# Single PSUM banks, other places and order of loads, six accumulators, and squares added on VectorE in a decoder layer's projections and gate

## The chip, the cores and the metric

One Trainium2 chip, of which the kernel uses one core. A core has TensorE (PE: matrix products; its weight loads, PEld, overlap them), VectorE (DVE), ScalarE (ACT), GpSimd (POOL) and SyncE (SP). TensorE writes its sums to PSUM, eight banks of 128 x 512 float32; VectorE and ScalarE read them from there. SP, POOL and ACT issue DMAs, each from a queue of its own in fixed order. The metric is the device time in microseconds (us) of one execution; less is better.

## What is computed

One layer over 1024 tokens of width 2048: norm, one projection to the columns of two attention groups, attention, output projection with residual, a gated embedding, a last norm. The change lies outside of attention:

```python
hn = rmsnorm(h, norm_mix_g[i])
proj = hn @ w_in[i]
...
mixed = jnp.concatenate([sb_out * jax.nn.silu(sb_g), df_out * jax.nn.silu(df_g)], axis=-1)
h = h + mixed @ w_out[i]
gate = jax.nn.sigmoid(rmsnorm(h, norm_ple_g[i]) @ w_ple_gate[i])
h = h + gate * (p[i] @ w_ple_proj[i])
return rmsnorm(h, norm_final_g)
```

All is float32. Activations lie transposed, features on partitions and 512 tokens (one half of the sequence) in a row, so a row block of 128 features is a tile of 128 x 512.

## The kernel before

**Products.** TensorE multiplies float32r, so each float32 operand is split into a high part (a cast, on ScalarE) and a low part (a subtraction, on VectorE), and each product is three matmuls: high x high, high x low, low x high. A group of four blocks of 128 is twelve matmuls of 128 x 512.

**Seven products for eight.** Three matrices (the columns for values and gates, the output projection, the gate) are multiplied by Winograd's scheme. The activations are cut by half of the tokens and half of the features into A11, A12, A21, A22, the weights likewise; seven products of sums are formed, named after their activation operand: A11, A12, S1 to S4 and A22. Operands S1 to S4 are formed ahead and kept in DRAM; weight sums (T1 to T4) are formed by VectorE from raw blocks 11, 12, 21, 22. For one output block (a unit `u`), A11 and A12 add up in accumulator `a`; S2, then S3 or A22, in `b`; S1, then S4, in `c`. Between, VectorE reads the partial sums: `u2 = b + s1` after S2 (L1225, L1867), `u3 = b + s1` after S3 (L1245, L1890), `o = c + u3` (L1247, L1897); after A22 into `b` and S4 into `c` come the last reads (L1169, L1791). A reader stands between two groups of matmuls into the same accumulator, so the second group waits for it.

**Stages.** To about 633 us: values and gates, 16 units in two phases (`ph`, halves of the features). To about 1655 us: projection of queries and keys, with attention of the previous head beside it. Then the output projection, 8 units in two phases, to about 1998 us; it stores rows of h (`h_d`) and their squares. Then the gate in three passes, where `gprod` (L1914) multiplies with all features at once (24 matmuls) for a unit:

- first pass: `p1(u)` multiplies A11 into accumulator `pa[u]` and stores the sum, `p2(u)` adds A12, and `gate1(u)` multiplies the embedding (`ple`: 6 matmuls into a tile `z`), scales `pa[u]` by the norm (`o`, L1996) and forms the new row of h. The order is written out: p1 0, 1, 2, p2 0, 1, norm, p1 3, p2 2, gate1 0, p1 4, gate1 1, p2 3, and so on.
- second pass: `p6` (S2), `p5` (S1) and `p3` (S4), in the order p6 0, p5 0, then for each u: p6 u+1, p3 u, p5 u+1.
- last pass: S3 and A22 of each unit for the other half of the tokens, with rows `q` and `h` read back from DRAM, the last norm, and the output rows. The tail after unit 5 works in halves of 256 tokens.

**PSUM.** Pool `pp` has two banks with the tag `acc` and two with `t`; pool `pz` has two tiles of two banks each. Attention takes a score tile `z` from it. In the projections one tile of `pz` is both `b` and `c` (L1221, L1862), except in every third unit of the first phase, where b and c are two `acc` tiles; in the gate, a single accumulator takes half of a tile of `pz` and leaves the other half empty. `pa[u]` lies in `acc` for u = 0, 1, 4, 5 and in `pz` for the others (L1979).

**Order.** The instructions of PE, VectorE and ScalarE stand in the order in which the program writes them. Each product is followed by `step()` (L828): it casts one further weight tile (`whigh` on ScalarE, L794; `wlow` on VectorE, L808 or L806), some five tiles ahead of its use, then runs what is due: operand splits from a list `xq` (two in a step), and functions put off by one to three steps (`soon`). Cast weights lie in a ring of ten tiles. DMAs on SP and POOL are ordered by a planner that simulates the program when it is built; `tc.issue_after(ins)` keeps a DMA behind `ins` on its queue.

**Loads of the gate.** Raw weights of the first pass come line by line into two buffers of two blocks (`first_load`, L1691; a line is A11 or A12 of a unit; the load for the line after next is asked for when a line is cast). For the second pass there are two sets of raw blocks; `second_diffs` (L1718) forms the sums of unit u and asks for the blocks of unit u+1, which take the buffers of unit u-1. Operands (8 rows of 256 KB for each name) are loaded where others have been used up: `GPLACE` (L1342) names the places (XP are pairs of tiles that held rows of x or of the projection's operands; FREE1 and FREE2 are attention's tiles v, pt, pt, q and q, k, k2, v2, which the projection's S3 and S1 used last), `NEXT` and `GNEXT` (L1345) the product after which they are asked for, with first row and count; `gate_loads` (L1368) puts their splits into `xq`. The squares of gate rows go to DRAM by a POOL DMA, two sums that accumulate there (`add_squares`, L1377), and are loaded again for the last norm (L2204).

Of the kernel before, what the change touches and what calls it, by code (L numbers as in the profile page):

```python
# [13 lines left out]
F32 = mybir.dt.float32  # L14
# [6 lines left out]
P = 128  # L21
D = 2048
S = 1024
HALF = 512
# [46 lines left out]
def _body(ctx, nc, tc, ap):  # L71
# [552 lines left out]
    with tc.tile_pool(name="at", bufs=2) as at, tc.tile_pool(name="pz", bufs=2, space=PSUM) as pz:  # L624
# [582 lines left out]
        for ph in range(2):  # L1207
            for u in range(2 * H):
# [117 lines left out]
        sq_d = dram.tile([3, 2, P, HALF], F32, name="sq_d", tag="sq_d")  # L1326
        SUMS = "S1", "S2", "S3", "S4"

        def load_operand(ph, nm, i, eng=nc.sync):
# [4 lines left out]
            if src is None:  # L1334
# [40 lines left out]
        nsq = [0, 0, 0, 0]  # L1375

        def add_squares(k, s):  # L1377


            n = nsq[k]  # L1380
            nsq[k] += 1
            G.dma_start(sq_d[k, n % 2], s, **(dict(accum_op=ALU.add) if n > 1 else {}))

        def row_squares(hf, o):
            n = nsq[3]
            nsq[3] += 1
            t = ev.tile([P, HALF], F32, name="rsq", tag=f"rstd{n % 2}", bufs=1)
            A.activation(t, o, AF.Square)
            add_squares(2 * hf, t)
# [79 lines left out]

        for half in (1, 0):  # L1470
# [200 lines left out]
        op.ticks = True  # L1671
        gneg = ev.tile([P, NK], F32, name="gneg", tag="zm", bufs=1)
# [45 lines left out]
        def second_diffs(u, ks):  # L1718
# [26 lines left out]
        for u in range(8):  # L1745
            for nm in ("S2", "S1", "S4"):
# [93 lines left out]
        for ph in range(2):  # L1840
            for u in range(8):
# [16 lines left out]
                elif ph == 1 and u == 7:  # L1858
                    b = pz.tile([P, 2, HALF], F32, name="pbc", tag="z")[:, 0, :]
                    c = None  # L1860
                else:
                    bc = pz.tile([P, 2, HALF], F32, name="pbc", tag="z")  # L1862
                    b, c = bc[:, 0, :], bc[:, 1, :]
# [27 lines left out]
                if ph:  # L1891
                    V.tensor_tensor(u3, u3, r[0, u + 8], op=ALU.add)
                    if u == 7:
                        c = pz.tile([P, 2, HALF], F32, name="pbc", tag="z")[:, 1, :]
# [14 lines left out]
        gate_loads("A12", 4)  # L1909

# [35 lines left out]
        def load_sums(half, tags):  # L1946
            r = []
            for i, (pool, tag, n) in enumerate(tags):
                r.append(pool.tile([P, HALF], F32, name="sums", tag=tag, bufs=n))
# [11 lines left out]
        def gating1(u, c, o, z):  # L1961
# [39 lines left out]
        p1(0)  # L2001
        p1(1)
        p1(2)
        op.calm = False
        embedding_load(1, "f")
        sums2 = load_sums(2, ((ev, "rstd1", 1), (ev, "ssq", 1)))
# [5 lines left out]
        plew_load(0, 0)  # L2012
        plew_load(1, 0)
# [3 lines left out]
        plew(0, 0)  # L2017
# [28 lines left out]
        def p6(u):  # L2046
# [8 lines left out]
            parts2[u] = pz.tile([P, 2, HALF], F32, name="pc", tag="z")[:, 0, :], w  # L2055
# [344 lines left out]
```

## Time and profile before

| | |
|---|---|
| median of 3 runs | 2388.85 us (2388.27 to 2389.63) |
| the profiled execution | 2393.9 us, span 2392.1 us |
| granted TensorE clock, mean | 0.992 |
| DMA | 590.46 MB, 247 GB/s |

By stage (busy us of each engine, and the mean share of the 16 DMA engines):

| stage, us | PE | DVE | ACT | DMA share |
|---|---|---|---|---|
| 53 to 633, values and gates | 574.5 of 580 | 404.1 | 218.8 | 0.88 |
| 633 to 1655, queries, keys, attention | 1007.2 of 1022 | 777.1 | 613.8 | 0.71 |
| 1655 to 1998, output projection | 334.7 of 343 | 273.0 | 149.7 | 0.89 |
| 1998 to 2104, gate, first pass | 100.0 of 106 | 65.2 | 53.4 | 0.91 |
| 2104 to 2257, gate, second pass | 148.6 of 153 | 114.0 | 56.9 | 0.92 |
| 2257 to 2392, gate, last pass and tail | 117.7 of 135 | 107.8 | 63.9 | 0.61 |

How to read what follows: times in rows count from the start of the span. In names, buffer numbers are left out, so `cgA12h` is the high part of a row of the gate's operand A12 (a name that ends in a digit, as cgS3, may be shown as cgS), `wpr` a cast weight tile, `wraw` a raw one, `pwhl` the split projection weights of the embedding. "PE x <- DVE y L1" is a wait of PE that ended with DVE's write of y at line 1. SPq is SP's queue of DMA issues. A table of stages gives, for each window, its length, then busy time and (x instructions) of PE, PEld, DVE, ACT and POOL, the granted clock, the DMA share and GB/s. Matmuls overlap, so their number says more than the busy time.

### The profile page before, as it was taken

The numbers are of one execution on the slowest core, as the hardware profiler recorded it, in microseconds if no ns is written. First come the engines' busy times: TensorE is split into PE (matmuls) and PEld (weight loads), VectorE is DVE, ScalarE is ACT, GpSimd is POOL, SyncE is SP. The second block draws the span as 40 slices with busy tenths as digits, with TensorE's granted clock in tenths as the row PEclk, the third lists the DMA queues.
The fourth block names the chain that finished last, engine by engine and source line by source line (L and its number), as shares of the span: only waits on it lengthen the run. The fifth ranks groups of instructions, "written<-read, shape, count | busy, mean of one in ns | idle before, by whom it ended". The sixth has DMA issues, their size and how long they took to land.

```text
span 2392.1 us, 32521 instructions
## 1 busy us (share of the span) xinstructions
PE 2332.3 (97%) x11102; PEld 1936.5 (81%) x11102; DVE 1781.2 (74%) x3107; ACT 1189.3 (50%) x2213; POOL 334.3 (14%) x497
## 2 busy tenths in 40 slices
PE   9999999999999999999999999999999999999997
PEld 7878878888788877887888888888878777778776
DVE  7489776666577787777888867768778886677687
ACT  6334243333366675445677764545634334533453
POOL 1211112323200000000011101101111231011000
PEclk9999999999999999999999999999999999999998
DMA  7798589999977788777656666668888899998955
GB/s 253 244 345 285 162 242 286 287 280 273 294 248 253 242 276 279 258 252 249 208 169 199 179 211 206 196 197 256 208 205 228 255 265 293 294 330 280 317 189 179
DMA packets 257510, 590.46 MB, mean 247 GB/s; under 512 B 29056, under 2 KB 41344, under 8 KB 257344
## 3 DMA queue, kind: packets, MB, share of 16 engines
q1 hardware_dynamic: 178384, 395.15, 48.8%
q0 software_dynamic: 59664, 158.10, 26.0%
q10 hardware_dynamic: 19296, 35.14, 4.3%
q8 instruction: 87, 1.43, 0.3%
q14 instruction: 79, 0.65, 0.1%
HBM read 374.37 MB, written 222.30 MB: 249 GB/s over the span
## 4 chain that ended last, share of the span: by engine, by line
PE 72%; DVE 11%; DMA 8%; ACT 7%; issue 2%; SPq 0%; ACTq 0%; DVEq 0%
PE acc L262 7%; PE acc L264 7%; PE acc L263 7%; PE pbc L703 6%; PE pbc L705 6%; PE pbc L704 6%; PE pa L705 2%; PE pa L704 2%; PE pa L703 2%; PE tp L481 2%; DMA wraw<-w_gate 1%; DMA wraw<-w_out 1%; PE pb L1918 1%; PE pb L704 1%; PE pb L705 1%
## 5 line engine op out<-in xcount | busy, mean ns | idle before, releaser
L794 ACT CAST wpr<-T 128x512 fp32r<-128x512 f32 x208 | 125.5, 620 | 442.9 <-DVE T L759 359.4
L262 PE MATMUL acc<-xh,whi 128*128 128x512 f32 x768 | 315.1, 410 | 0.0
L264 PE MATMUL acc<-xh,wlo 128*128 128x512 f32 x768 | 302.3, 394 | 1.1 <-DMA wlo<-wlo_d 1.1
L263 PE MATMUL acc<-xl,whi 128*128 128x512 f32 x768 | 301.0, 392 | 0.0
L264 PEld LDWEIGHTS acc<-xh,wlo 128*128 128x128 f32 x768 | 144.4, 188 | 35.0 <-DMA wlo<-wlo_d 2.3
L263 PEld LDWEIGHTS acc<-xl,whi 128*128 128x128 f32 x768 | 145.5, 189 | 24.0
L262 PEld LDWEIGHTS acc<-xh,whi 128*128 128x128 f32 x768 | 145.0, 189 | 23.8 <-DVE qk L1549 0.4
L794 ACT CAST wpr<-wraw 128x512 fp32r<-128x512 f32 x144 | 88.3, 616 | 148.3 <-DMA wraw<-w_gate 36.8
L808 DVE TENSOR_TENSOR wpr<-T,wpr 128x512 fp32r<-128x512 f32 x208 | 142.8, 686 | 13.1 <-ACT wpr L794 9.2
L927 POOL DMA_DIRECT2D vg_d<-hc x120 | 86.8, 724 | 344.1 <-DVE hc L1169 206.7
L808 DVE TENSOR_TENSOR wpr<-wraw,wpr 128x512 fp32r<-128x512 f32 x144 | 97.9, 686 | 38.6 <-ACT wpr L794 38.5
L504 DVE TENSOR_TENSOR awl<-tp,awh 128x256 fp32r<-128x256 f32 (+1 forms) x160 | 92.5, 578 | 43.0 <-ACT awh L499 42.2
L499 ACT CAST awh<-tp 128x256 fp32r<-128x256 f32 (+1 forms) x160 | 80.6, 503 | 82.6 <-PE tp L481 76.4
L322 DVE CUSTOM_DVE_ANT_0 z<-z,masks 128x512 f32<-128x512 f32 (+7 forms) x128 | 97.1, 769 | 22.9 <-PE z L342 13.8
L703 PE MATMUL pbc<-cS,wpr 128*128 128x512 f32 x288 | 112.2, 389 | 0.8 <-DVE u L1225 0.8
L705 PE MATMUL pbc<-cS,wpr 128*128 128x512 f32 x288 | 112.1, 389 | 0.0
L704 PE MATMUL pbc<-cS,wpr 128*128 128x512 f32 x288 | 112.0, 389 | 0.0
L374 DVE TENSOR_TENSOR_SCAN st<-pt 128x511 f32<-128x511 f32 (+3 forms) x64 | 86.7, 1354 | 27.5 <-ACT pt L367 27.0
L367 ACT ACTIVATE pt<-z 128x512 f32<-128x512 f32 (+3 forms) x64 | 41.8, 653 | 76.9 <-DVE z L350 74.9
L529 PE MATMUL av<-awl,v 128*128 128x256 f32 x256 | 73.5, 287 | 2.0 <-DVE awl L504 2.0
L527 PE MATMUL av<-awh,v 128*128 128x256 f32 x256 | 72.0, 281 | 0.7 <-ACT awh L499 0.7
L528 PE MATMUL av<-awh,v 128*128 128x256 f32 x256 | 72.2, 282 | 0.0
(570 smaller groups left out, 6831.8 us busy)
## 6 DMA issues: line engine op xcount, KB each, us to landing
wlo<-wlo_d SPq DMA_DIRECT2D x94, 512.0 KB, 5.1
whi<-whi_d SPq DMA_DIRECT2D x74, 512.0 KB, 4.0
wraw<-w_vg SPq DMA_DIRECT2D x130, 256.0 KB, 4.6
vg_d<-hc POOLq DMA_DIRECT2D x120, 256.0 KB, 5.5
wraw<-w_in SPq DMA_DIRECT2D x54, 512.0 KB, 5.3
wraw<-w_gate SPq DMA_DIRECT2D x92, 256.0 KB, 5.4
wraw<-w_out SPq DMA_DIRECT2D x72, 256.0 KB, 4.8
wlo_d<-wlo SPq DMA_DIRECT2D x34, 512.0 KB, 3.4
```

The lines of the kernel that those rows point to most:

```text
L262: T.matmul(acc[c], hi[:, k2, kh, c, :], xh, start=first, stop=False)
L263: T.matmul(acc[c], hi[:, k2, kh, c, :], xl, start=False, stop=False)
L264: T.matmul(acc[c], lo[:, k2, kh, c, :], xh, start=False, stop=last)
L322: V.tensor_tensor_reduce(z, z, mwide[:, 0:n], -DF_SCALE, 3.0e38, ALU.add, ALU.min, mx)
L374: V.tensor_tensor_scan(st[:, off + 1:nkey], pt[:, off:nkey - 1], pt[:, off:nkey - 1], initial=1.0, op0=ALU.mult, op1=ALU.bypass)
L504: V.tensor_tensor(wl[:, o, :], tp[:, o, :], wh[:, o, :].bitcast(F32), op=ALU.subtract)
L703: T.matmul(o, wh[:, w], xh, start=start and k == 0, stop=False, skip_group_check=True)
L704: T.matmul(o, wh[:, w], xl, start=False, stop=False, skip_group_check=True)
L705: T.matmul(o, wl[:, w], xh, start=False, stop=k == 3, skip_group_check=True)
L794: A.copy(t[:, 0], src)
L808: V.tensor_tensor(t[:, 1], src, t[:, 0].bitcast(F32), op=ALU.subtract)
L927: G.dma_start(vg_d[hf, blk, u], o, **(dict(accum_op=ALU.add) if ph else {}))
```

## The change

- **Single banks.** Outside of attention four tiles of one bank (`single`) replace the two tiles of two banks: the eight accumulators at the start, b and c in both projections, the accumulators of the gate. The pool of pairs is opened for attention alone.
- **Six accumulators.** `pa[u]` of units 2 to 5 takes a single bank, 0, 1, 6 and 7 take `acc`.
- **Places and order of operands.** A11's and S1's upper rows lie in XP[8:12] and those of A12 and S4 in FREE1, the other way round than before; `NEXT` and `GNEXT` follow.
- **Second pass.** S4 of units 0 and 1 comes after S1 of unit 1, in the list of weights; on PE, p5 1 comes ahead of p3 0. Block 22 of unit 2 is asked for when unit 0's S4 has been cast.
- **Embedding.** Its first projection weights are loaded after p1 0 and split after p1 2.
- **Squares.** Those of gate rows are added by VectorE into a constant's tile that attention used (`spare32`); the DMAs, the loads and one of the two tiles in the last norm go.
- **Last pass.** Two h and two q rows are loaded ahead instead of four and three; loads of pw, h, q and final rows stand behind the last one noted (`op.loaded`), to which the weights of the last pass now belong.

```diff
-    with tc.tile_pool(name="at", bufs=2) as at, tc.tile_pool(name="pz", bufs=2, space=PSUM) as pz:
+    with tc.tile_pool(name="at", bufs=2) as at, ExitStack() as banks:
+        def singles(name):
+            banks.close()
+            pool = banks.enter_context(tc.tile_pool(name=name, bufs=4, space=PSUM))
+            return lambda nm: pool.tile([P, HALF], F32, name=nm, tag="z")
+
+        single = singles("pv")
...
-        for _ in range(2):
-            z = pz.tile([P, 2, HALF], F32, name="paz", tag="z")
-            aa += [z[:, 0, :], z[:, 1, :]]
+        aa += [single("paz") for _ in range(4)]
...
-                    bc = pz.tile([P, 2, HALF], F32, name="pbc", tag="z")
-                    b, c = bc[:, 0, :], bc[:, 1, :]
+                    b, c = single("pbc"), single("pbc")
...
-        GPLACE = {"A11": XP[0:4] + FREE1, "A12": XP[4:12], "S2": FREE2 + [("at", t) for t in ("k", "k2", "v2", "v")],
-                  "S1": XP[12:16] + FREE1, "S4": XP[4:12], "S3": XP[0:4] + FREE2, "A22": XP[12:16] + XP[8:12]}
-
-        NEXT = {"A11": [("A11", 0)], "S3": [("A11", 4, 3)], "S1": [("A11", 7, 1), ("A12", 0)]}
+        GPLACE = {"A11": XP[0:4] + XP[8:12], "A12": XP[4:8] + FREE1, "S2": FREE2 + [("at", t) for t in ("k", "k2", "v2", "v")],
+                  "S1": XP[12:16] + XP[8:12], "S4": XP[4:8] + FREE1, "S3": XP[0:4] + FREE2, "A22": XP[12:16] + XP[8:12]}
+
+        NEXT = {"A11": [("A11", 0)], "S2": [("A11", 4, 3)], "S3": [("A11", 7, 1)], "S1": [("A12", 4, 3), ("A12", 0)]}
         GNEXT = {("A11", 1): [("S1", 4)], ("A12", 0): [("S4", 0)], ("A12", 1): [("S4", 4)],
-                 ("S2", 1): [("S3", 4)], ("S1", 1): [("A22", 0)], ("S4", 1): [("A22", 4)]}
+                 ("S2", 1): [("S3", 4)], ("S1", 1): [("A22", 0), ("A22", 4)]}
...
+        spare32 = masks.bitcast(F32)[:, 0:HALF]
...
+        banks.close()
+        pz = banks.enter_context(tc.tile_pool(name="pz", bufs=2, space=PSUM))
         for half in (1, 0):
...
         op.ticks = True
+        single = singles("pr")
...
-                nc.sync.dma_start(w, tw_d[u, int(nm == "A22")])
+                op.loaded = nc.sync.dma_start(w, tw_d[u, int(nm == "A22")])
...
         def second_hook(u, ks):
+            if u == 0:
+                second_load(2, ks, 22)
...
                 for b in (12, 11, 22, 21):
-                    second_load(u + 1, ks, b)
+                    if (u, b) != (1, 22):
+                        second_load(u + 1, ks, b)
...
-        for u in range(8):
-            for nm in ("S2", "S1", "S4"):
+        for u, nms in [(0, ("S2", "S1")), (1, ("S2", "S1")), (0, ("S4",)), (1, ("S4",))] + [(u, ("S2", "S1", "S4")) for u in range(2, 8)]:
+            for nm in nms:
...
         def plew_load(u, c):
...
-                nc.sync.dma_start(pws[u, c], ap["w_pp"][u][:, :, c, :])
+                with tc.issue_after(op.loaded.ins):
+                    nc.sync.dma_start(pws[u, c], ap["w_pp"][u][:, :, c, :])
...
-        gate_loads("A12", 4)
+        gate_loads("A12", 7, 1)
...
                 t = hc.pop(u + 8 * c)
-                A.activation(o, t, AF.Square)
+                if u + c == 0:
+                    A.activation(spare32, t, AF.Square)
+                else:
+                    A.activation(o, t, AF.Square)
+                    V.tensor_tensor(spare32, spare32, o, op=ALU.add)
                 A.dma_start(h_d[1, u + 8 * c], t)
-                add_squares(1, o)
...
-            if u % 4 > 1:
-                pa[u] = pz.tile([P, 2, HALF], F32, name="paz", tag="z")[:, 0, :]
+            if 1 < u < 6:
+                pa[u] = single("paz")
...
         p1(0)
+        plew_load(0, 0)
+        plew_load(1, 0)
         p1(1)
         p1(2)
+        plew(0, 0)
...
         for u in range(8):
             p6(u + 1)
+            if u == 0:
+                p5(1)
...
-                p5(u + 1)
+                if u:
+                    p5(u + 1)
...
-        for u in range(4):
+        for u in range(2):
             load_h(u)
-        qs = {u: load_q(u) for u in range(3)}
+        qs = {u: load_q(u) for u in range(2)}
...
-            if u < 5:
-                qs[u + 3] = load_q(u + 3)
-            load_h(u + 4)
-            if u == 0:
-                sums1 = load_sums(1, ((ev, "rstd1", 1), (ev, "sq", 2)))
-            elif u == 1:
-                norm(sums1)
-            else:
+            qs[u + 2] = load_q(u + 2)
+            load_h(u + 2)
+            if u == 1:
+                norm([spare32])
+            elif u > 1:
```

More of the change, by code (lines that the diff above doesn't have):

```diff
@@ L1325, in _body @@
         q_d = dram.tile([8, 2, P, HALF], F32, name="q_d", tag="q_d")
-        sq_d = dram.tile([3, 2, P, HALF], F32, name="sq_d", tag="sq_d")
+        sq_d = dram.tile([2, 2, P, HALF], F32, name="sq_d", tag="sq_d")
         SUMS = "S1", "S2", "S3", "S4"
@@ L1893, in _body @@
                     if u == 7:
-                        c = pz.tile([P, 2, HALF], F32, name="pbc", tag="z")[:, 1, :]
+                        c = single("pbc")
                         prod(u, ph, "S1", c, True)
@@ L1944, in norm, with load_sums @@
             op.soon.extend([(op.slot + 1, roots), (op.slot + 2, step)])
-        def load_sums(half, tags):
+        def load_sums(half):
             r = []
-            for i, (pool, tag, n) in enumerate(tags):
-                r.append(pool.tile([P, HALF], F32, name="sums", tag=tag, bufs=n))
+            for i, tag in enumerate((f"rstd{half}", "ssq")):
+                r.append(ev.tile([P, HALF], F32, name="sums", tag=tag, bufs=1))
                 op.loaded = nc.sync.dma_start(r[i], sq_d[half, i])
@@ L2054, in p6 @@
             G.dma_start(q_d[u, 0], w)
-            parts2[u] = pz.tile([P, 2, HALF], F32, name="pc", tag="z")[:, 0, :], w
+            parts2[u] = single("pc"), w
         def p5(u):
@@ L2102, in load_h @@
                 hpair[u] = at.tile([P, 2, HALF], F32, name="h0", tag=HP[u], bufs=BUFS.get(HP[u], 2))
-                nc.sync.dma_start(hpair[u], h_d[0].rearrange("(a k) p t -> k p a t", a=2)[u])
+                with tc.issue_after(op.loaded.ins):
+                    nc.sync.dma_start(hpair[u], h_d[0].rearrange("(a k) p t -> k p a t", a=2)[u])
         def load_q(u):
@@ L2109, in load_q @@
                 r.append(xp.tile([P, HALF], F32, name="qt", tag=f"x{'hl'[i]}{KT[4 + u % 4]}"))
-                nc.sync.dma_start(r[i], q_d[u, i])
+                with tc.issue_after(op.loaded.ins):
+                    nc.sync.dma_start(r[i], q_d[u, i])
             return r
@@ L2134, in final1 @@
             t = ftile()
-            nc.sync.dma_start(t, h_d[1, ch])
+            with tc.issue_after(op.loaded.ins):
+                nc.sync.dma_start(t, h_d[1, ch])
             def fn():
-                V.scalar_tensor_tensor(t, t, gvec[:, 2, ch:ch + 1], sums1[0], op0=ALU.mult, op1=ALU.mult)
+                V.scalar_tensor_tensor(t, t, gvec[:, 2, ch:ch + 1], spare32, op0=ALU.mult, op1=ALU.mult)
                 nc.sync.dma_start(ap["out"][ch * P:ch * P + P, HALF:], t)
@@ L2173, in begin @@
             V.tensor_tensor(q2, bs[u], q2, op=ALU.add)
-            zs[u] = pz.tile([P, 2, HALF], F32, name="ple", tag="z")[:, 0, :]
+            zs[u] = single("ple")
             z = pp.tile([P, HALF], F32, name="z1", tag="t")
@@ L2214, in _body @@
         W = {(u, nm, ks): op.wq.pop((u, "g" + nm, ks)) for u in (6, 7) for nm in ("S3", "A22") for ks in range(2)}
-        z = {u: pz.tile([P, 2, HALF], F32, name="ple", tag="z") for u in (6, 7)}
+        z = {(u, c): single("ple") for u in (6, 7) for c in range(2)}
         Q = HALF // 2
@@ L2284, in _body @@
         for c in (1, 0):
-            ple(0, 6, c, z[6][:, c, :])
+            ple(0, 6, c, z[6, c])
         begun(6, 1, 0)
@@ L2289, in _body @@
         for c in (1, 0):
-            ple(0, 7, c, z[7][:, c, :])
+            ple(0, 7, c, z[7, c])
         begun(7, 1, 0)
```

27 lines of the change are left out of this document (10 added, 17 removed).

## The prediction

> **What bounds the kernel now.** First the page: which engine is busy all the time.
>
> ```profile
> PE 2332.3 (97%) x11102; PEld 1936.5 (81%) x11102; DVE 1781.2 (74%) x3107; ACT 1189.3 (50%) x2213; POOL 334.3 (14%) x497
> ```
>
> TensorE (PE) is the bound, and the diff leaves out only two of its matrix products (the norm of one tile). So the change can win only time in which PE waits. Hence next the waits of PE, for the two stretches that the diff touches: 60 to 700 us (the value and gate projection), then 1742 to 2360 us (output projection and gate). Columns: us in total, times, longest.
>
> ```profile
> PE pbc L703 <- DVE hc L1247: 3.5, 2, 2.5
> PE pbc L703 <- DVE hc L1169: 1.3, 2, 0.8
> PE pbc L703 <- DVE u L1225: 0.8, 1, 0.8
> ```
>
> ```profile
> PE z L1836 <- ACT pwhl L1828: 3.6, 2, 2.2
> PE pbc L703 <- DVE hq L1897: 2.3, 3, 0.9
> PE pb L1920 <- DVE wpr L808: 1.9, 1, 1.9
> PE pc L1918 <- DVE hc L2061: 1.7, 2, 1.2
> PE pa L1918 <- DVE o L1996: 1.6, 1, 1.6
> PE pb L1918 <- DVE qt L2196: 1.4, 1, 1.4
> PE pa L1918 <- ACT cgA12h L681: 1.1, 1, 1.1
> PE pb L1918 <- DVE qt L2173: 0.6, 1, 0.6
> ```
>
> Some 20 us in all. A wait costs more than its idle time, so I also counted matmuls, in the table of stages; read the x behind PE's busy time, the granted clock (third from the end) and the DMA share (second from the end).
>
> ```profile
> 2020.00:2030.00 10.00, 9.12 (x35) 6.67 (x36) 7.92 (x12) 5.00 (x9) 0.00 (x0) 1.00 0.68 243
> 2040.00:2050.00 10.00, 6.94 (x28) 5.00 (x28) 6.36 (x11) 4.16 (x9) 0.00 (x0) 1.00 0.83 269
> 2100.00:2110.00 10.00, 7.81 (x28) 6.03 (x27) 6.67 (x12) 4.58 (x9) 0.84 (x1) 0.83 1.06 376
> 2120.00:2130.00 10.00, 8.30 (x28) 6.41 (x29) 9.96 (x17) 5.03 (x10) 2.03 (x3) 0.83 0.84 252
> 2140.00:2150.00 10.00, 10.00 (x46) 8.29 (x45) 5.98 (x11) 1.88 (x3) 2.02 (x3) 1.00 1.00 286
> 2240.00:2250.00 10.00, 8.96 (x36) 6.39 (x35) 8.83 (x15) 7.36 (x13) 0.00 (x0) 1.00 1.02 375
> 2280.00:2290.00 10.00, 8.68 (x38) 7.22 (x39) 9.55 (x16) 6.44 (x13) 0.00 (x0) 1.00 0.58 204
> 2060.00:2130.00 70.00, 65.48 (x272) 52.88 (x271) 49.88 (x83) 31.86 (x60) 6.87 (x9) 0.95 0.99 326
> ```
>
> An unbroken 10 us holds 46 matmuls (2140), 10 / 46 = 0.22 us each. The four windows of the gate's first two passes lack 11, 18, 18 and 18: 65 x 0.22 = 14.3 us. Two of the last pass lack 10 and 8: 2.2 and 1.8 us. In two windows the granted clock is 0.83, and the chain shows why.
>
> ```profile
> 2105.60 0.43 PE z L1837
> ...
> 2108.48 0.23 PE pb L1920
> ```
>
> After its 2.2 us wait PE issues a matmul each 0.43 us for nearly 3 us before it is back at 0.23. A long wait is paid almost twice. The Trainium skill's page "TensorE: Matmul & The Clock Gate", section "What's actually happening", says that the array falls to half clock after an idle window of about 3.4 us; by that rule alone a wait of 2.2 us would cost only itself, and the windows at 2100 and 2120 about 4 us together instead of 8. Here the row speaks against so long a threshold.
>
> **The change part by part.** I price against the profiled execution (2393.9 us, span 2392.1).
>
> *Single banks (L624, L989, L1221, L1862).* b and c were halves of one two-bank tile.
>
> ```profile
> 1856.73 0.61 DVE u L1890
> ...
> 1858.84 0.50 PE pbc L703
> ```
>
> ```profile
> 178.04 0.61 DVE u L1245
> ...
> 179.42 0.60 PE pbc L703
> ```
>
> The waiting product at 1858.84 is A22, which adds into b. L1890, the read of b, ended at 1857.34; PE waited 1.5 us more, until L1897 had read c. At 179.42 likewise: the read of b (L1245) ended at 178.65, PE waited for L1247, which reads c. So PE waits for readers of the other half, and no wait of this kind stands against `pb`, the single tiles of every third unit. Separate tiles take it away. Total of those waits: 3.5 + 1.3 + 0.8 + 2.3 = 7.9 us. What is late next is the bank's own reader: in the longest (2.5 us, so from 176.9) that is 178.65, so 1.7 us stay, and I leave 0.4 for the others: gain **5.8**. Bounds: 0 (if the tile isn't what is waited for) to 7.9. Closing and opening pools around attention happens twice; if a new tile has to wait there, the nearest row is an hq wait (0.9 at most): 0 to 2 lost, I take 0, since both places lie behind other PE work.
>
> *Places and order of the gate's operands, first pass.* The wait for cgA12h (1.1 us) begins in SP's queue.
>
> ```profile
> 2004.47 9.26 SPq L1691 DMA_DIRECT2D wraw<-w_gate  x4
> 2013.90 0.33 SPq L1950 DMA_DIRECT2D sums<-sq_d  x1
> 2014.34 0.37 SPq L1361 DMA_DIRECT2D cgA12l<-h_d  x1
> ```
>
> A12's last row stands behind four weight loads that wait 9 us for their buffers. Now A12's rows 4 to 6 go to places that are free after S1 and only one row is left after the projection; A11's upper rows go out one product earlier (S2 instead of S3). Same DMAs, same bytes, one row fewer behind the weights: of the 11 missing matmuls (2.4 us) about 1 us is the norm's own work, the rest, **1.4**, goes. Bounds 0 to 2.4.
>
> *Six accumulators, projection weights of the embedding early.* Window 2040 holds the o L1996 wait (1.6: unit 4's accumulator is unit 0's, still unread) and one of the two pwhl waits (3.6 - 2.2 = 1.4). Unit 4 now has its own bank, and the cast of pwhl is issued before the norm. Next late would be unit 6, which takes unit 0's bank four products later. Of 18 x 0.22 = 4.0 I take **3.5**; bounds 0 to 4.0. The moved cast and its two loads of 128 KB run beside the first three products.
>
> *Window 2100* (pwhl 2.2 plus slow clock, 4.0 in all) hangs on S1's upper rows, loaded when A11's last product ends; they change place together with A11, so this moment stays. I take **0.5**; bounds -1 (unit 0's second-pass tile now needs the bank of unit 6, read late) to 4.0.
>
> *Order of S4 (L1745, L2076 to L2091, L1727).* pb L1920 waits for DVE wpr L808: unit 1's S2 weights, cast after unit 0's S4 in the list but used before it. In the new order the two agree through unit 1, and S4 no longer stands right behind the read of its c (hc L2061, 0.5 of the 1.7 us here). Gain of the 4.0: **3.8**; bounds 1 to 4. In return unit 2's block 22 is loaded only after S4's cast, two products later; its user follows two products (24 x 0.22 = 5.3 us each) on, and that covers a landing.
>
> *Squares on VectorE.*
>
> ```profile
> L1965 DVE TENSOR_TENSOR hc<-hc,o 128x512 f32<-128x512 f32 x15 | 10.4, 692 | 0.5
> ```
>
> ```profile
> sq_d<-o POOLq DMA_DIRECT2D x16, 256.0 KB, 7.3
> ```
>
> Fifteen adds of the shape of L1965 put 15 x 0.69 = 10.4 us on VectorE, spread over some 200 us beside PE's products: 0, and up to 2 where VectorE is full (9.96 of 10 us at 2120). Sixteen DMAs of 256 KB (all but two accumulate) leave POOL's queue and the DMA engines, whose share is 0.99 from 2060 to 2130; this shortens landings there. I count it as cover for the terms above, not as a term.
>
> *Last pass.*
>
> ```profile
> 2252.60 8.99 SPq L2110 DMA_DIRECT2D qt<-q_d  x6
> 2261.69 0.38 SPq L1363 DMA_DIRECT2D cgA22l<-h_d  x1
> ```
>
> ```profile
> 2295.21 1.72 PE ssps L1931 x4
> ```
>
> A22's upper rows wait behind six q loads. After the change they are asked for one product earlier, with two h and four q loads ahead instead of four and six (2 x 512 + 2 x 256 KB less), and a load of h, q, pw or a final row may no longer overtake the weights (issue_after). Behind such a held load stand the next weights and the output rows on SP; its users come at least one product later. The waits on qt (1.4 + 0.6) go: **2.0**, bounds 0 to 2.3. The gap at 2240 (hc L2061, 1.2) stays: S4 of unit 7 still follows S1 directly. The norm sums one tile instead of two: 1.72 / 2 = **0.9**, surely; its two loads go too.
>
> Sum: 5.8 + 1.4 + 3.5 + 0.5 + 3.8 + 2.0 + 0.9 = 17.9. 2393.9 - 17.9 = 2376.0. The median of the runs, 2388.85, is 5.05 below the profiled execution: **2371 us**. With every term at its upper bound: 7.9 + 2.4 + 4.0 + 4.0 + 4.0 + 2.3 + 0.9 = 25.5, so 2363. With half the terms: about 2380.
>
> **Rivals.**
>
> *DMA is full, and moving loads only displaces others.* For it: shares of 0.99 from 2060 to 2130, 1.06 at 2100, 1.02 at 2240. If the stage's bytes set its pace, PE's earlier arrival is paid back at the next load. Then the first pass keeps its waits but for the order of S4, and half of the last pass's: 5.8 + 3.8 + 1.0 + 0.9 = 11.5, less 2 for the projection, whose loads would also come late: 9.5, so 2379. Against it: 0.68 and 0.83 at 2020 and 2040, where most of the loss is, and the sixteen DMAs that go. The Trainium skill's page "DMA: Bandwidth & Descriptors", section "Issuing engines are not separate DMA queues", says that transfers issued by SP, ACT and POOL run on the same sixteen engines and interleave; by that rule reordering wins no bandwidth, and only the dropped DMAs do.
>
> *The single banks don't do what they say:* PE's waits pass to the bank's own readers. 17.9 - 5.8 = 12.1, so 2377. Against it: `pb` never waits so.
>
> *Slower: the weights' double buffer becomes the bound in the gate's first pass.*
>
> ```profile
> 2042.99 1.28 SPq L1691 DMA_DIRECT2D wraw<-w_gate  x2
> ...
> 2057.12 1.04 SPq L1691 DMA_DIRECT2D wraw<-w_gate  x2
> ```
>
> A buffer comes round in 14.1 us, and serves two lines; PE needs for an A11 and an A12 line 48 matmuls and 6 of the embedding, 54 x 0.23 = 12.4. Today casts made ahead cover the 1.7. If the accumulators let PE run ahead, the cover is used up; with one add more (0.7) each of eight rounds costs 2.4: 19 us, and the first pass gives nothing. Net 19 - 5.8 - 2.0 - 0.9 = 10 slower: 2399. It decides from the point where all rounds exceed 12.4 us and no line lies cast ahead; against it speaks that PE stands at 46 per 10 us in 2140 with a DMA share of 1.00.
>
> **Chances.** Forecast 0.62 (2363 to 2377), full DMA 0.23, banks without effect 0.06, slower 0.05; 0.04 for gains that cancel to nothing. A measurement of this kernel tells about 0.2% (4.8 us) from no change. Faster: 0.62 + 0.06 + most of 0.23 = 0.88; same 0.06; slower 0.06. The range of 8 in 10 runs from just under the sum of upper bounds to past the full-DMA case with its restarts: **2361 to 2383**.
>
> **What would show it.** Right: no wait of pbc for L1247 or L1897's successors in the list of PE's waits, at most the own readers'; no wait of pa for o; 46 matmuls in the windows that hold units 4 and 1's S2; ssps x2. Wrong: waits of the same size on cgA12h, pwhl or wpr some products later with a DMA share of 1.0 (rival one), weights' rounds over 12.4 us with PE waiting for wpr (slower), or a new wait of pb for o at the start of the second pass. The forecast fails most easily in the terms 3.5 and 3.8, which suppose that what stands behind the removed wait is ready.

## The result, and the profile after

The kernel after takes **2370.95 us** (median of 6 executions, 2367.97 to 2374.04), the kernel before, beside it on the same chip, 2388.20 (6 executions): ratio 0.993, 95% interval [0.9917, 0.9943]. Measured once more in a later group, the same kernel took 2367.84 (2364.25 to 2370.06), ratio 0.9912 [0.9898, 0.9925]. All ten executions have a median of 2370.0. So the change is 17 to 21 us faster; the prediction was 2371 in 2361 to 2383.

The profiled execution took 2367.97 us, its span is 2366.2 us. The page's line of engines, as before the prediction:

```profile
PE 2319.3 (98%) x11100; PEld 1929.7 (82%) x11100; DVE 1787.5 (76%) x3122; ACT 1188.8 (50%) x2213; POOL 320.1 (14%) x481
```

The waits of PE, from 60 to 700 us and then from 1742 to 2360 us (us in total, times, longest):

```profile
PE pbc L709 <- DVE u L1248: 2.7, 2, 2.0
PE pb L709 <- DVE u L1248: 0.9, 1, 0.9
```

```profile
PE z L1841 <- ACT pwhl L1833: 3.2, 2, 2.3
PE ssps L2276 <- DVE sq L2265: 1.5, 1, 1.5
PE pbc L709 <- DVE u L1894: 1.0, 2, 0.6
PE pa L1921 <- ACT cgA12h L687: 0.9, 1, 0.9
PE pbq L2241 <- DVE qt L2248: 0.4, 1, 0.4
```

No `pbc` waits for `hc` or `hq` any more, the readers of the other half; what is left waits for its own bank's reader (`u`). The waits on o, qt of the full rows, wpr and hc are gone. The two waits on pwhl and the one on a split row of A12 are there as before. The one on `ssps` isn't new: it belongs to the tail, which in the kernel before lies past 2360 us.

Where the time came from is read best from the start of each stage's first matmul. The table gives the length of each stage in the profiled executions: two of the kernel before (its own, and one of the first experiment), two of the kernel after (its own, and one of its repetition).

| stage, us | before | after | mean difference |
|---|---|---|---|
| values and gates | 620.1, 618.0 | 615.0, 616.5 | -3.3 |
| queries, keys, attention (no edit in it but pools opened) | 1028.4, 1030.4 | 1026.5, 1027.5 | -2.4 |
| output projection, first phase | 111.3, 111.9 | 106.3, 106.3 | -5.3 |
| output projection, second phase | 161.7, 163.3 | 159.8, 160.9 | -2.2 |
| gate, first pass | 109.8, 108.4 | 106.4, 104.6 | -3.6 |
| second pass up to the last S1 | 134.1, 135.8 | 129.5, 129.3 | -5.6 |
| last S1 and S4 | 15.5, 14.2 | 14.0, 14.0 | -0.9 |
| last pass, first five products | 39.3, 39.2 | 35.8, 35.8 | -3.4 |
| the rest of it, and the tail | 95.8, 95.7 | 96.7, 97.2 | +1.3 |

The second phase of the output projection and the gate's first pass have to be read together. Five traces have the banks, accumulators, places and embedding loads of the kernel after: its own two and those of the experiments on the order of S4, the squares and the last pass. In them the phase took 158.3 to 162.0 us and the pass 103.3 to 107.6, but both together 265.3 to 266.2: where PE comes to the gate later, it waits less there. In the two traces of the kernel before both together took 271.5 and 271.7.

With the lead-in and the start of the output projection's operands, which didn't change, the spans are 2392.1 and 2392.9 against 2366.2 and 2368.3: 25.3 us in the mean. That is more than the 17 to 21 us between the medians. Both profiled executions of the kernel before lie above its median, by 5 and 6 us; those of the kernel after lie 3 below and 2 above theirs. The other executions left no trace, so in which stage they were shorter stays open.

### The profile page after: what moved, and what is told of

Its sections match the earlier page's. It is cut to its first block, busy times and chain, and to the rows that moved or that the text cites. A ratio compares the mean times of both kernels' runs of the same rounds, so it can differ in the third digit from the quotient of the medians.

```text
span 2366.2 us, 32488 instructions
## 1 busy us (share of the span) xinstructions
PE 2319.3 (98%) x11100; PEld 1929.7 (82%) x11100; DVE 1787.5 (76%) x3122; ACT 1188.8 (50%) x2213; POOL 320.1 (14%) x481
## 4 chain that ended last, share of the span: by engine, by line
PE 71%; DVE 10%; DMA 9%; ACT 7%; issue 3%; POOL 0%; ACTq 0%; SPq 0%; DVEq 0%; POOLq 0%
PE acc L264 7%; PE acc L262 7%; PE acc L263 7%; PE pbc L709 6%; PE pbc L710 6%; PE pbc L711 6%; PE pa L709 2%; PE pa L710 2%; PE pa L711 2%; PE tp L481 2%; PE pb L1923 1%; PE pb L1921 1%; PE pb L1922 1%; DMA spare<-xT 1%; PE pc L1923 1%
```

## The experiments

All times are medians, with the range and the ratio to the kernel before in the same group. "After" is 2370.0 us, the ten executions together.

| kernel | us | range | ratio to before [95%] |
|---|---|---|---|
| before again | 2388.22 | 2383.74 to 2394.64 | 0.9996 [0.9987, 1.0006] |
| before, single banks | 2386.09 | 2379.1 to 2388.1 | 0.9984 [0.9975, 0.9993] |
| after, pairs of banks | 2376.11 | 2370.63 to 2380.52 | 0.9943 [0.9931, 0.9955] |
| after, old order of S4 | 2373.89 | 2370.43 to 2375.65 | 0.9933 [0.9921, 0.9944] |
| after, embedding loads untied | 2374.74 | 2372.57 to 2375.99 | 0.9936 [0.9923, 0.9948] |
| after, four accumulators | 2371.06 | 2369.52 to 2372.61 | 0.9922 [0.9909, 0.9935] |
| after, old places | 2368.74 | 2365.66 to 2371.36 | 0.9911 [0.9896, 0.9925] |
| after, old last pass | 2368.72 | 2365.6 to 2378.8 | 0.992 [0.9901, 0.9938] |
| after again | 2367.84 | 2364.25 to 2370.06 | 0.9912 [0.9898, 0.9925] |
| after, squares by DMA | 2373.85 | 2366.6 to 2384.83 | 0.994 [0.9921, 0.996] |
| after, embedding weights ahead | 2370.44 | 2367.36 to 2373.08 | 0.9923 [0.991, 0.9937] |
| the same, and A12's row 7 in turn | 2369.84 | 2364.33 to 2376.11 | 0.9919 [0.9902, 0.9936] |

### How far a span can be trusted: both kernels once more

The kernel before, unchanged:

> The kernel before once more, unchanged. Theory (the gain is the sum of PE waits that the diff takes away): ratio to before 1.000 within 0.0015, and a second trace of it has the same waits as the first except where a load was late by chance: the 4.5 us wait for a w_out block at 1738 us (first phase of the output projection), which the changed kernel's trace has at 1.1 us though no edit touches it, is then under 2 us, and the profiled time lies near 2388 instead of 2393.9. Rival (a side effect of the change mended that wait, and it belongs to the gain): the wait is 4 to 5 us here too.

The kernel after, unchanged, in the last group:

> The kernel after once more, unchanged, beside the others of this group. Theory: its median lies where the first six executions had it, 2370 to 2372, with the same waits of the matmul queue (pwhl 3.2 in two, wpr in the output projection 1.1); then the 2368.7 of the kernels with the old places and with the old last pass is a difference of about 2. Rival: medians of five move by 2 us from group to group, and it comes out at 2368 to 2369.5: then the two were level with it.

The wait for the w_out block (next experiment) was there again, 4.9 us; that it came and went by chance, my first theory, fell. The median of the kernel after came out at 2367.84: the rival. Medians of four to six executions move by 3 us from group to group, so the kernels in the table between 2367.8 and 2371.1 aren't told apart by their times. In all fourteen traces the attention, in which nothing was edited, took between 1026.3 and 1032.3 us. A stage that an edit doesn't touch thus moves the span by up to 6 us. In what follows an edit of a few us is judged by its stage first, and by the time only where that is clear.

### A wait that I hadn't priced: the block of w_out

The first phase of the output projection became 5 us shorter, and no term of the prediction stands there. The chain of the kernel before, at the start of that phase:

```profile
1725.98 10.60 DMA wraw<-w_out
1736.66 0.70 DVE T L759
1737.38 0.70 DVE T L759
1738.11 0.63 ACT wpr L794
1738.78 0.50 PE pbc L703
1739.51 0.77 PE pbc L705
1740.28 0.43 PE pbc L703
```

And that of the kernel after:

```profile
1719.02 7.14 DMA wraw<-w_out
1726.28 0.70 DVE T L765
1727.01 0.70 DVE T L765
1727.73 0.63 ACT wpr L800
1728.40 0.50 PE pbc L709
1728.90 0.23 PE pbc L710
```

The same load lands 3.5 us sooner, and the matmuls behind it run at 0.23 us at once, where they took 0.43 us before. What went out on SP's queue just ahead of it in the kernel before:

```profile
1721.09 1.28 SPq L1822 DMA_DIRECT2D pw<-w_pp  x2
1722.48 0.54 SPq L291 DMA_DIRECT2D mixed_d<-sg  x1
1723.07 0.55 SPq L1822 DMA_DIRECT2D pw<-w_pp  x1
1723.71 0.78 SPq L750 DMA_DIRECT2D wraw<-w_out  x1
1724.53 1.25 SPq L1822 DMA_DIRECT2D pw<-w_pp  x2
1725.98 11.72 SPq L750 DMA_DIRECT2D wraw<-w_out  x4
```

Five loads of the embedding's weights, first used some 300 us later, were put there because their buffers had just come free. The change ties them behind a load that is issued later (`issue_after`), and in the trace after the first goes out at 1990.2 us. The experiment takes that tie away and leaves the rest of the change:

```diff
-                with tc.issue_after(op.loaded.ins):
-                    nc.sync.dma_start(pws[u, c], ap["w_pp"][u][:, :, c, :])
+                nc.sync.dma_start(pws[u, c], ap["w_pp"][u][:, :, c, :])
```

> The kernel after, but with the loads of the embedding weights (pw<-w_pp) no longer tied behind the last load that the code issued before them, so that five of them go out ahead of the w_out block on which the output projection's first product stands, as in the kernel before. Theory: these five loads (128 KB each, in small pieces) were what held that block up; pbc<-ACT wpr goes from 1.1 back to 4 to 5 us, the block's load from 7.1 to 10 us or more, the first matmuls behind it are at 0.43 us again, and the time is 3.5 to 5 us above the kernel after (2374.5 to 2376), less what earlier weights save at the waits for pwhl in the gate (4.3 us in all, read apart in the trace). Rival: the block came sooner because the attention ended sooner and met other transfers; then the wait stays at 0.7 to 1.2 us and the time within 1.5 us of the kernel after.

The five loads were back in their old place, and so was the wait:

```profile
1723.29 11.02 DMA wraw<-w_out
...
1736.51 0.80 PE pbc L709
1737.31 0.43 PE pbc L710
```

The phase took 112.05 us. In the ten traces with the tie it took 105.8 to 107.0 us, in the three others without it 111.0 to 111.9. Part of this comes back in the gate, where PE waited for pwhl for 0.5 us instead of 3.2 and 2.5: the second phase and the gate's first pass together took 263.5 us, 1.8 to 2.7 less than in the five traces above. The theory holds: one tie on a queue wins more than 5 us, 270 us ahead of where the tied loads now go out, and by this one trace some 3.5 of them are left behind the gate's first pass. The time, 4.7 us above the kernel after (3.8 and 6.9 above its two medians), points the same way.

### Single banks

In the kernel before alone, only the projections' pairs became single banks (the accumulators at the start, b and c); then the kernel after got its pairs back in the same places:

```diff
...
-                    bc = pz.tile([P, 2, HALF], F32, name="pbc", tag="z")
-                    b, c = bc[:, 0, :], bc[:, 1, :]
+                    b, c = single("pbc"), single("pbc")
...
```

> The kernel before with single banks for b and c in both projections and for the eight accumulators at the start, and nothing else of the change; the gate keeps pairs. Theory (PE waited for readers of the other half): 5 to 7 us faster than before, no wait of pbc for L1247 or L1897 (reads of c), what is left waits for the reads of b (u, L1245 and L1890) or is gone. Rival (the waits pass to the bank's own readers, or the late loads of the output projection take the time back): 0 to 2 us faster, PE's waits on pbc of 7 us in all as before.

> The changed kernel with pairs again for b and c in both projections and at the start; single banks stay in the gate. Theory: 5 to 7 us slower than the changed kernel (2376 to 2378), the waits for readers of c are back with about 8 us in all, and the gate runs as in the changed kernel. Rival (banks have no effect): 2371 as the changed kernel.

With pairs the waits for the other half's readers are back in the kernel after (60 to 700 us, then 1742 to 2010 us):

```profile
PE pbc L713 <- DVE hc L1257: 3.1, 2, 1.6
PE pbc L713 <- DVE hc L1179: 1.3, 2, 0.8
PE pbc L713 <- DVE u L1235: 0.8, 1, 0.8
```

```profile
PE pbc L713 <- DVE hq L1909: 2.4, 5, 0.7
```

With single banks in the kernel before they are gone, and what is left from 60 to 700 us waits for the bank's own reader:

```profile
PE pbc L709 <- DVE u L1248: 1.9, 3, 0.8
```

By time the edit was worth 2.5 us in the kernel before (its group's median of the kernel before is 2388.61; 3.8 by the ratio, 1.7 to 6.0 by its interval), and 6 in the kernel after. By stages, the three traces with pairs took 618.6 us in the mean for values and gates and 162.7 for the second phase of the output projection, the eleven with single banks 616.1 and 160.7: 4.4 us together, though the single lengths overlap (617.8 to 620.1 against 613.7 to 618.9 for values and gates). In the kernel after with pairs the second phase and the gate's first pass together took 270.0 us, 3.9 to 4.8 more than in the five traces above, so part of the loss stands behind the phase itself. The mechanism is shown; its size lies between 2.5 and 6, in the kernel before below the 5 to 7 of the theory.

### The order of S4

The kernel after with the list of weights, p5 1 and block 22 of unit 2 in the old order:

```diff
...
-        for u, nms in [(0, ("S2", "S1")), (1, ("S2", "S1")), (0, ("S4",)), (1, ("S4",))] + [(u, ("S2", "S1", "S4")) for u in range(2, 8)]:
-            for nm in nms:
+        for u in range(8):
+            for nm in ("S2", "S1", "S4"):
...
```

> The changed kernel with the old order of the second pass: S4 of unit 0 in the list ahead of unit 1's S2, p3 0 ahead of p5 1, block 22 of unit 2 asked for with the others. Theory: 3 to 4.5 us slower than the changed kernel; PE waits for wpr (the low part of unit 1's S2 weights) 1 to 2 us at the third product of the pass and 0.5 us for the read of c after it. Rival (the DMAs of the squares, which are gone here as well, made those weights late): at most 1 us slower, no wait for wpr.

The waits came back in the second pass (2080 to 2140 us):

```profile
PE pb L1920 <- DVE wpr L814: 3.0, 2, 2.3
PE pc L1918 <- DVE hc L2064: 1.6, 1, 1.6
```

The pass up to the last S1 took 134.8 us. The four traces with the old order lie at 134.1 to 135.8, the ten with the new one at 129.2 to 130.3: the order is worth 5.2 us by the means. The time lies 3.9 us above the kernel after, 2.9 and 6.0 above its two medians; it points the same way, but alone it wouldn't settle the size.

### Six accumulators

```diff
-            if 1 < u < 6:
+            if u % 4 > 1:
                 pa[u] = single("paz")
```

> The kernel after, with the gate's first pass back at four accumulators (units 0, 1, 4 and 5 in the two banks tagged acc, 2, 3, 6 and 7 in single banks). Theory: the six accumulators alone carry the stretch from the product A12 of unit 2 to A11 of unit 4, which became 3.8 us shorter in the trace; the time is 3 to 4 us above the kernel after (2374 to 2375) and the loss stands in that stretch. Rival: once each bank is tracked by itself and the embedding weights are loaded early, four accumulators are enough: under 1 us, 2370 to 2372.

The wait that the six accumulators took away is there again, larger than before (1995 to 2100 us):

```profile
PE pa L1921 <- DVE o L2002: 3.0, 1, 3.0
```

From unit 2's A12 to unit 4's A11 the trace lost 3.2 us, as in the theory. From the last A12 to the second pass it won something back: 6.8 us with four accumulators, 8.0 to 10.0 in the five traces with six. PE came there later, and the cast of pwhl was ready. The first pass by itself, 107.7 us against 106.4 and 104.6, says little, since PE came to it late, after a second phase of 162.0 us. With that phase it took 269.7 us, 3.5 to 4.5 more than in the five traces: as much as the theory says, in one trace. The time doesn't confirm it: 0.1 and 3.2 us above the two medians of the kernel after. So the mechanism is shown, its size in the time is open, and the rival isn't ruled out by the time.

### Places and order of the gate's operands

`GPLACE`, `NEXT` and `GNEXT` as before, and all four upper rows of A12 loaded after the projection:

> The kernel after, with the places and the order of the gate's operands (and the rows of A12 loaded ahead) as in the kernel before. Theory, from the trace: this part only moved the wait for a split A12 row from row 7 to row 3 and is worth nothing: 2369.5 to 2372.5, with the wait for a cgA12h row of 1 to 3 us at row 7 again and none at row 3. Rival, my prediction's term: 1.4 us (0 to 2.4) above the kernel after, 2372.4 to 2373.4.

The time was 1.3 us below the kernel after, within its scatter. The wait in the first pass, with the old places and, below, with the new (1980 to 2030 us):

```profile
PE pa L1921 <- ACT cgA L687: 1.1, 1, 1.1
```

```profile
PE pa L1921 <- ACT cgA12h L687: 0.9, 1, 0.9
```

The same wait stands in both. In the kernel after, A12's last row still goes out behind the weights, and its split is put in front of those of rows 0 to 3, so ScalarE waits for its load and PE for row 3. In the repetition of the kernel after, the wait for cgA12h wasn't there: it hangs on when the gate begins against its loads. With the old places the second phase and the gate's first pass together took 267.5 us, 1.3 to 2.2 more than in the five traces above; that would be the prediction's term, but it is one trace, and the time says the opposite. A gain from this part is not shown, nor is it ruled out.

### Squares by DMA

The kernel after with the squares summed by accumulating DMAs again, and two tiles in the norm:

```diff
...
-                if u + c == 0:
-                    A.activation(spare32, t, AF.Square)
-                else:
-                    A.activation(o, t, AF.Square)
-                    V.tensor_tensor(spare32, spare32, o, op=ALU.add)
+                A.activation(o, t, AF.Square)
                 A.dma_start(h_d[1, u + 8 * c], t)
+                n = len(n1)
+                n1.append(0)
+                G.dma_start(sq_d[2, n % 2], o, **(dict(accum_op=ALU.add) if n > 1 else {}))
...
```

> The kernel after, with the squares of the gate's rows summed again by accumulating DMAs on GpSimd's queue, loaded before the last pass, and normed from two tiles. Theory, my prediction's terms: the sum on VectorE is worth nothing by itself, the shorter norm 0.9 us: 0.5 to 1.5 us above the kernel after of this group, with the step between products 4 and 5 of the last pass 0.9 us longer. Rival: the 16 accumulating transfers less are what made the operands of the last pass land sooner, and the gap of 1.8 us ahead of the last product S4 comes back as well: 2.5 to 3.5 us above it.

The norm cost 0.86 us, to the point. And the gap ahead of the last S4 came back (15.6 us for the last S1 and S4, instead of 14.0). The operands of the last pass on ScalarE, in this kernel and in the kernel after:

```profile
2217.65 1.40 ACT L687 ACTIVATE cgS<-cgS,gvec 128x512 fp32r<-128x512 f32 x2 [9.13 <-DMA cgS<-hcomb_d]
```

```profile
2214.14 1.34 ACT L687 ACTIVATE cgS<-cgS,gvec 128x512 fp32r<-128x512 f32 x2 [5.93 <-DMA cgS<-hcomb_d]
```

and their loads in the 27 us around it (KB each, median us to landing), again this kernel first:

```profile
cgS3l<-hcomb_d SPq DMA_DIRECT2D x4, 256.0 KB, 6.8
cgS<-hcomb_d SPq DMA_DIRECT2D x4, 256.0 KB, 7.9
```

```profile
cgS3l<-hcomb_d SPq DMA_DIRECT2D x4, 256.0 KB, 3.7
cgS<-hcomb_d SPq DMA_DIRECT2D x4, 256.0 KB, 5.6
```

Late operands make late casts; VectorE's low parts stand behind them, and behind these VectorE's read of the bank that S4 adds into. In the kernel before, too, ScalarE had waited 9.59 us for these rows.

The other traces bound this. The four loads `cgS<-hcomb_d` took 6.9 to 8.5 us (medians) in all four traces with the DMAs and 5.4 to 6.6 in all ten without. But the gap opened only where the last row landed after the last S1 had begun, 1.1 us in the kernel before and 0.9 here (15.5 and 15.6 us for the last S1 and S4); in the two other traces with the DMAs it was there as that S1 began, and the two products took 14.2 and 14.4. So no wait of PE shows a cost of the adds on VectorE, 15 x 0.69 us beside its work, and the DMAs that they replace cost from 0.2 to 1.6 us, as the rows land. The time, 3.9 us above the kernel after, has a wide range (2366.6 to 2384.8).

### The last pass

Four h and three q pairs ahead, and nothing tied:

> The kernel after, with the last pass's loads of h rows, q rows and final rows as before: four h pairs and three q pairs ahead, nothing tied behind an earlier load. Theory: the waits for qt come back, 1.5 to 2.5 us above the kernel after (2372.5 to 2373.5), all of it behind the second pass. Rival: the qt waits went because everything before reaches the last pass at another time, and the order there is worth under 0.8 us (2370 to 2371.8).

In its trace the first five products of the last pass took 38.35 us against 35.83 in the nine other traces that have the new order and the single norm: 2.5 us, as in the theory. The waits (2230 to 2290 us) are on the weights and on A22's rows, no longer on qt:

```profile
PE pb L1921 <- ACT wpr L800: 1.5, 1, 1.5
PE pb L1922 <- DVE cgA22l L693: 0.4, 1, 0.4
```

The times don't show it: a median of 2368.72 in a range of 13 us. By the stage this part is worth 2.5 us; by the time it is inconclusive.

### Can more be had: the waits for pwhl

Both waits for pwhl come from casts that stand on ScalarE behind splits whose rows are late. One unit ahead they should be free (loads and casts of the first pass; then, in a second kernel, also A12's row 7 split in its turn):

```diff
-            plew_load(*((u + 2, 0) if u < 6 else (u - 6, 1)))
+            if u < 7:
+                plew_load(*((u + 3, 0) if u < 5 else (u - 5, 1)))
...
-            plew(*((u + 1, 0) if u < 7 else (0, 1)))
+            if u < 7:
+                plew(*((u + 2, 0) if u < 6 else (0, 1)))
...
+        plew_load(2, 0)
...
+        plew(1, 0)
...
-            if nm in ("A11", "A12") and i0 > 3:
+            if nm in ("A11", "A12") and i0 > 3 and (nm, i0) != ("A12", 7):
```

> The kernel after, with the embedding weights of the gate's first pass loaded and cast one unit ahead (the first still behind the output projection's loads). Theory: the two waits for pwhl (3.2 us, and the stretch from the last A12 to the first S2 of the second pass, 9.4 us, which is 2.5 us over its work) go, no other takes their place: 2 to 3.5 us below the kernel after of this group. Rival: ScalarE's casts were only the last of several things that came late; the operands of S4 or a block of w_gate are late next, and under 1 us is won.

> As the kernel with the embedding weights ahead, and the split of A12's last row in its turn, behind the splits of rows 0 to 3, instead of in front of them. Theory: the wait for a split A12 row in the first pass (0.9 and 0.3 us) goes too: 1 to 1.5 us below the kernel with the embedding weights ahead alone, 3 to 5 below the kernel after of this group. Rival: row 7 is then late at its own product, as it was before the change (1.2 us there), and nothing is won beside the other kernel.

The waits for pwhl went, and the one on cgA12h in the second kernel. In both another came, which the chain of the first shows:

```profile
2080.54 6.05 DMA wraw<-w_gate
2086.61 0.33 ACTq L1735
2086.98 0.59 ACT s L1991
2087.61 0.50 PE pa L1921
```

A store on ScalarE's queue (L1735) waits for a late block of w_gate; behind it stands ScalarE's copy of A11's sum out of the accumulator, and A12 of that unit waits for the copy. It cost 2.3 us of the 3.7 that went. The first pass came to 105.1 and 101.2 us; with the phase before it that is 264.8 and 265.6, at most 1 us below the five traces' 265.8 in the mean, and neither time is below the kernel after's. The rival of the first holds: the cast was one of several things that came late there. No version of these experiments is shown to beat the kernel after.

## Why the prediction was right, and where it wasn't

The number was right, and the sum behind it only in part. By its steps:

- **What bounds the kernel:** right. PE stays the bound, 98% busy, and all that was won is time in which PE waited.
- **Single banks, 5.8 (0 to 7.9):** the mechanism as put there, readers of the other half; own-bank readers (`u`) are late next, as expected, for 0.9 us also at `pb`, which in the kernel before never waited so. 2.5 to 6 us.
- **Places and order of operands, 1.4 (0 to 2.4):** not shown, though one trace would allow it (1.3 to 2.2). I saw one row fewer behind the weights and took the wait to go; but the last row is enough for it, and its split now stands ahead of four others.
- **Six accumulators, 3.5, and window 2100, 0.5:** the stretch that I priced became 3.8 us shorter in both traces of the kernel after, and the trace without the six loses 3.5 to 4.5 up to the second pass; the time shows 0 to 3. The wait in window 2100 stays (2.2 us before, 2.3 in the trace of the kernel after); only the half clock behind it went. The whole first pass, for which my terms make 5.4, won 3.6 us, and with the phase before it 5.8. The step that failed there is that I put the tie on the embedding's loads at nothing in this pass: by the one trace without it, it takes 1.8 to 2.7 us back up to the second pass, and PE waits less for pwhl there.
- **Order of S4, 3.8 (1 to 4):** right as a mechanism, and too small: 5.2.
- **Squares, 0, and "the gap at 2240 stays":** wrong. I counted the sixteen DMAs as cover for other terms; they delay the last pass's operands, and with them this gap opens in two of the four traces that have the DMAs: 0.2 to 1.6 us.
- **Last pass, 2.0, and norm, 0.9:** right, 2.5 and 0.86 in their stage.
- **Not in the sum:** the block of w_out, 5 us, of which some 3.5 are left behind the gate's first pass. I read the waits of PE from 1742 us on, since the edits' lines begin there, and the wait ended at 1738.8. The prediction names the tie on loads of pw in the last pass only, and never asked where those loads stood before.
- **Not in the sum, against it:** the stretch from the sixth product of the last pass to the end is 1.3 us longer; in the tail PE now waits for qt (0.4 and 0.9 us in the two traces).

Against the traces the sum was too small, 17.9 of 25.3. By the table of stages the rest comes from the w_out block (5.3), an attention that differs by 2.0 between the two executions of the kernel before alone (2.4), S4 (1.8 over its term), the last S1 and S4 (0.9) and the last pass with its norm (0.5 over), less what the gate's first pass (1.8), the tail (1.3) and the single banks (0.3) stayed short. Against the median it was right because I took it from the median, while the two profiled executions of the kernel before lie 5 and 6 us above theirs. So 2371 is partly two errors that cancel: a wait that I missed, and a difference of traces that the medians show only in part. That the sum met the median is, so far, luck.

Of the rivals, "DMA is full" held in places, not over the whole: at the squares, at the weights ahead, and at the end of the gate's first pass, which the five traces reach within 0.9 us of each other, counted from the start of the phase before, whether PE comes to the pass early or late. "Banks without effect" and the slower case fell: no wait for a cast weight tile (`wpr`) stands in the gate's first pass, which became shorter.

## What to carry to other kernels

When an edit ties a load behind another, look up where that load went out before: a planner puts a load where its buffer comes free, and that may be just ahead of the one that everything waits for. Read the waits from well before the first edited line. And price waits in a chain, not one by one: where the next wait ends at a load, PE's earlier arrival only makes it longer (here a spread of 3.7 us at the start of the gate's first pass was one of 0.9 at its end), so take such stages together; and before believing a sum of terms of 1 to 3 us, see how much a stage without edits moves between executions (here up to 6 us).

## What the runs showed of the hardware that I had not expected

- **A wait of the same length is paid once or twice.** The chains of the kernel before, after 2.2 us without a matmul, and the kernel after, after 2.3 us, both waiting for pwhl:

```profile
2104.81 0.79 PE z L1836
2105.60 0.43 PE z L1837
```

```profile
2088.69 0.50 PE z L1841
2089.18 0.24 PE z L1842
```

  The table of stages gives a granted clock of 0.50 from 2106 to 2108 us in the one and 1.00 throughout in the other. I had taken the first for the rule. The Trainium skill's page "TensorE: Matmul & The Clock Gate", section "What's actually happening", says that the gate watches a window of about 3.4 us that is free-running and doesn't reset when a kernel starts, and that half clock comes after at least one idle window. That the same wait falls on either side agrees with a free-running window, and so does the length of the half clock in the trace of the kernel before, 3.41 us from 2104.79 us. The idle window doesn't fit: the 3.41 us ahead of that moment held 1.24 us of matmuls and only 2.17 us without.
- **Loads issued just ahead delay a load that is waited for.** Five loads of 128 KB ahead of a block of 256 KB moved its landing from 7.1 (6.7 with the old order of S4) to 10.6 and 11.0 us.
